# Third-block products behind X and Y, split bk transposes, filler ahead of chunk 0, modulation sums on VectorE

## The chip, the core and the metric

The kernel runs on one core of a Trainium2 chip. The metric is the device time of one execution in microseconds (us). The core has TensorE (PE, with its weight loads PEld), VectorE (DVE), ScalarE (ACT), GpSimd (POOL) and SyncE (SP, which issues the DMAs). TensorE's granted clock is shown as a share of full speed: 1.00 is 2.4 GHz, 0.50 is 1.2 GHz.

## The reference, cut to what matters

Two layers; each runs three token mixers on the same normalised input and merges them. 1024 latent and 256 context tokens, width 1024, all in float32.

```python
mod = silu(cond) @ w_mod + b_mod                       # 3072 sums for x, as many for ctx: the modulation
shift, scale, gate = split(mod, 3)
h = rms_norm(x, g) * (1 + scale) + shift               # h @ w_in gives all streams of the three mixers
# A: RWKV-7, both directions, 8 heads of 64
S_t = S_{t-1} (diag(w_t) - kk_t^T (a_t kk_t)) + v_t^T k_t ;  y_t = S_t r_t
# B: y = B * conv3(C * u)      C: differential attention, 4 heads, two softmax maps each
x = x + gate * (sum_i sigmoid(g_i) * (y_i * silu(z_i)) @ w_branch_i) @ w_out
```

## The kernel before, in words

Every large product is made of three fp32r products (high and low halves): a group of 24 products of 128x512 or 128x256 for one PSUM tile `pjt`, recorded at L158. A weight block of 256 columns arrives as two `wraw` loads, ScalarE rounds it to `whi` and VectorE subtracts to `wlo` (`split`, L111 to L113).

A layer runs in this order. `proj_stage` (L319) makes r, k, v, the decays and the q and k of attention, and ends with the conv stage (L563 to L593): four blocks `pr`, each with `u` and `cu` groups and then `gb` and `z` groups. `mod_next` (L553) is called once per token group there and works off one of 24 modulation blocks in layer 0 (8 in layer 1). One block is a 128x1024 load `wm`, eight products (L252) with `sc32` as weights that put four partial sums into four partition groups of `pjt`, a copy to `mr` on VectorE (L258), and a small product with `sel2` (L262, the fold) that adds the four, deferred behind the next group.

`rwkv_stage` (L597) is the chunked scan: 20 chunks of 64 tokens, both directions and all heads at once, on small products recorded at L148. For a chunk c:

- `prep(c, d)` (L642) makes the products `pa` of k and r with b and k, masks them to `mb` on VectorE (L656), and ScalarE copies the diagonal blocks to `dg` (L662).
- `turn_b(c)` (L664) transposes `bkT` through the PSUM tile `pt` into `bk`, four products and one ScalarE copy per direction.
- `solve(c)` (L675) inverts the unit triangular 32x32 diagonal blocks on VectorE: two transposes `dgT` and `at`, then some forty short steps on `P` and `R` (the first writes `P` at L702), and the transposes `tt` and `tn` (L720, L723).
- `corner(c)` (L729) makes the third, off-diagonal 32x32 block of the inverse: W from `mb` and `tn` on PE, a copy `ws` on ScalarE, Z from `ws` and `tt` on PE, a copy into `ti`.
- `chain(c)` (L748): X and Y products of the old state, then U from `ti` and X, then D and the second Y products, and the new state S on VectorE.

Buffers matter here. `dgT`, `R` and `tn` share one buffer (tag R); `P` and `ws` share one (tag P); W, Z and `pt` share one PSUM bank (tag pt, pool `pre`); U has a bank of its own (tag U, pool `chn`); `bk` has two buffers.

The loop (L809 to L832) interleaves the steps of chunk c with the solve of c + 1 and the preparation of c + 2. Between them `fill` (L1244) issues steps of projections that later stages need: `vd_fill`, `z_fill`, then `g_fill`, as a rule six products (a quarter of a group) per step. `PACE[l]` sets how many steps a call takes (7 in two calls, in layer 1 3 in one) and, as its third number, how many are left to attention, which spreads them over its own steps (L1256). A scheduler orders the instructions of each engine from the program, so the order below differs a little from the code. Each engine then takes its instructions in that order.

Of the kernel before, what the change touches and what calls it, by code (L numbers as in the profile page):

```python
# [23 lines left out]
FTH = 1  # L24
VDE = ((0,), ())
PJB = (0, 3)
PACE = ((7, 2, 184), (3, 1, 107))


B_LW, B_KR, B_V, B_QD, B_KD, B_VD, B_UC, B_GZ, B_ZA, B_ZC, B_G = 0, 1, 5, 7, 9, 11, 13, 17, 21, 23, 25  # L30
# [9 lines left out]
def tile_backbone(ctx: ExitStack, tc: tile.TileContext, xT_in, cond_in, w_mod, vecs, w_in, d_up, a_up,  # L40
# [88 lines left out]
    def defer(f, n=1):  # L129

        late.append([n, f])
# [108 lines left out]
        hv.append(small.tile([128, NV], F32, name=f"hv{l}"))  # L240
        ve.tensor_scalar(out=hv[l], in0=vec[l], scalar1=0.5, scalar2=None, op0=ALU.mult)

    def mod_stage(l, blocks, tags=(("wm", 1),), behind=False):
        prev = None
        for x, b in enumerate(blocks):
            ps = pj_tile()
            tag, nb = tags[x % len(tags)]
            raw = wp.tile([128, 8, 128], F32, tag=tag, name="wm", bufs=nb)
            dma.dma_start(out=raw, in_=w_mod[l, b])
            for k in range(8):  # L250
                g = k % 4
                i = te.matmul(out=ps[32 * g:32 * g + 32, 0:128], lhsT=sc32[:, k, :], rhs=raw[:, k, :],  # L252
                              start=(k < 4), stop=(k >= 4), skip_group_check=True)
            if prev is not None:
                with tc.issue_after(i.ins):
                    prev()
            mr = small.tile([128, 128], F32, tag="mr", name="mr", bufs=2)
            ve.tensor_copy(out=mr, in_=ps[:, 0:128])  # L258

            def fold(b=b, ps=ps, mr=mr):  # L260
                pm = ps[:, 128:130]
                te.matmul(out=pm, lhsT=mr, rhs=sel2, start=True, stop=True)  # L262
                m = modT[l][:, b, :]
                ve.tensor_scalar(out=m, in0=pm, scalar1=vec[l][:, V_BM + b:V_BM + b + 1], scalar2=None, op0=ALU.add)
                if 8 <= b < 16:
                    ve.tensor_scalar(out=G[l][:, b - 8, :], in0=m, scalar1=1.0,
                                     scalar2=vec[l][:, V_NG + b - 8:V_NG + b - 7], op0=ALU.add, op1=ALU.mult)
                elif b >= 16:
                    ve.tensor_scalar(out=m, in0=m, scalar1=0.5, scalar2=None, op0=ALU.mult)

            if behind:
                defer(fold)
            else:
                prev = fold
        if prev is not None:
            prev()

# [41 lines left out]
    def proj_stage(l, lowp, les, w):  # L319
# [233 lines left out]
        def mod_next():  # L553
            if mods:
                m, mb_ = mods.pop(0)
                mod_stage(m, [mb_], behind=True)

        hvl = hv[l]

# [37 lines left out]
    def rwkv_stage(l, fill):  # L597
# [63 lines left out]
                    s = slice(64 * (1 - p) + 32 * q, 64 * (1 - p) + 32 * q + 32)  # L661
                    se.copy(out=dg[s, d], in_=mb[s, d, p, :, 32 * q:32 * q + 32])  # L662

        def turn_b(c):  # L664
            if c >= 20:
                return
            bkT = bkTs.pop(c)
            bk = bks[c] = rp.tile([128, 2, 4, 128], F32, tag="bk", name="bk", bufs=2)
            for d in range(2):
                pt = pre.tile([128, 4, 128], F32, tag="pt", name="pt")  # L670
                for pr in range(4):
                    te.transpose(out=pt[:, pr, :], in_=bkT[:, 4 * d + pr, :], identity=ident)
                se.copy(out=bk[:, d], in_=pt)

        def solve(c):  # L675

# [52 lines left out]
        def corner(c):  # L729

            if c >= 20:
                return
            mb, (tt, tn) = mbs[c], tts.pop(c)
            W = pre.tile([128, 4, 128], F32, tag="pt", name="W").rearrange("p a (b i) -> p (a b) i", i=32)[:, 0:8, :]
            run_mm([(W[blk(p, 1), 4 * d + pr, :], mb[blk(p, 0), d, p, pr, 32:64], tn[blk(p, 0), 4 * d + pr, :], True, True)
                    for d, pr, p in units])
            ws = rp.tile([128, 4 * 7 * 28], F32, tag="P", name="ws", bufs=1)[:, 0:256].rearrange("p (u i) -> p u i", i=32)
            for p in range(2):
                se.copy(out=ws[blk(p, 1)], in_=W[blk(p, 1)])
            yield  # L740
            Z = pre.tile([128, 4, 128], F32, tag="pt", name="Z").rearrange("p a (b i) -> p (a b) i", i=32)[:, 0:8, :]
            run_mm([(Z[blk(p, 0), 4 * d + pr, :], ws[blk(p, 1), 4 * d + pr, :], tt[blk(p, 1), 4 * d + pr, :], True, True)
                    for d, pr, p in units])
            for p in range(2):
                se.copy(out=ti[blk(p, 0), :, 32:64], in_=Z[blk(p, 0)])
            yield

        def chain(c, S, yst):  # L748
            y, kr, mb, uv = has_y(c), krs.pop(c), mbs.pop(c), uvs[c]
            X = chn.tile([128, 2, 4, 64], F32, tag="XD", name="X")  # L750
            Y = chn.tile([128, 2, 4, 64], F32, tag="Y", name="Y") if y else None
            first = lambda d, pr: d == 0 and pr == 0
            calls = [(X[half[1 - p], d, pr, :], mb[half[p], d, p, pr, 0:64], uv[half[p], d, p, pr, :], first(d, pr), False)
                     for d, pr, p in units]
            for d, pr, p in units:
                kc, sv = kr[half[p], 4 * d + pr, :], S[half[p], d, pr, :]
                calls.append((X[half[1 - p], d, pr, :], kc[:, 0:64], sv, False, False))
                if y:

                    calls.append((Y[half[p], d, pr, :], sv, kc[:, 64:128], first(d, pr), False))  # L760
            run_mm(calls)
            x1 = rp.tile([128, 2, 4, 64], F32, tag="xs", name="xs", bufs=1)
            se.copy(out=x1, in_=X)
            yield
            U = chn.tile([128, 2, 4, 64], F32, tag="U", name="U")
            run_mm([(U[half[1 - p], d, pr, :], ti[half[1 - p], 4 * d + pr, :], x1[half[1 - p], d, pr, :], True, True)
                    for d, pr, p in units])
            for p in range(2):
                se.copy(out=uv[half[1 - p], :, p], in_=U[half[1 - p]])
            yield  # L770
            bk = bks.pop(c)
            D = chn.tile([128, 2, 4, 64], F32, tag="XD", name="D")
            calls = [(D[half[p], d, pr, :], bk[:, d, pr, half[p]], uv[:, d, p, pr, :], True, True) for d, pr, p in units]
            if y:
                calls += [(Y[half[p], d, pr, :], uv[:, d, p, pr, :], mb[:, d, p, pr, 64:128], False, True)
                          for d, pr, p in units]
            run_mm(calls)
            Sn = rp.tile([128, 2, 4, 64], F32, tag="S", name="S", bufs=2)
            ve.tensor_tensor(out=Sn, in0=D, in1=S, op=ALU.add)
            ve.tensor_tensor(out=f8(Sn), in0=f8(Sn), in1=dd_all[0][:, c, :].unsqueeze(2).to_broadcast([128, 8, 64]),  # L780
                             op=ALU.mult)
            if y:
                i = c % 2
                se.copy(out=yst[:, 0, :, 64 * i:64 * i + 64], in_=Y[:, 0])
                se.copy(out=yst[:, 1, :, 64 - 64 * i:128 - 64 * i][:, :, ::-1], in_=Y[:, 1])
                if i:
                    w = c // 2
                    for d, tb in enumerate((1024 + 128 * w if w < 2 else 128 * w - 256, 1152 - 128 * w)):
                        dma.dma_start(out=yd_dr[l][d][:, :, tb:tb + 128], in_=yst[:, d])
            uvs.pop(c)  # L790
            yield Sn
# [5 lines left out]
        load_b(1)  # L797
        load_k(1)
        load_v(0)
        for c in range(2):  # L800
            prep(c, 0)
            prep(c, 1)
            turn_b(c)
            if c == 0:
                for _ in solve(0):
                    fill()
                cor = corner(0)
                next(cor)
        load_b(2)  # L809
        for c in range(20):  # L810
            if c % 2 == 0:
                yst = rp.tile([128, 2, 4, 128], F32, tag="yst", name="yst", bufs=1)
            load_v(c + 1)
            load_k(c + 2)
            load_b(c + 3)
            steps, sol = chain(c, S, yst), solve(c + 1)
            next(steps)
            next(cor)
            next(sol, None)
            fill()  # L820
            next(steps)
            prep(c + 2, 0)
            next(sol, None)
            fill()
            S = next(steps)
            prep(c + 2, 1)
            next(sol, None)
            turn_b(c + 2)
            next(sol, None)
            fill()  # L830
            cor = corner(c + 1)
            next(cor, None)  # L832
        es.close()

    def vd_fill(l, b, sp):
# [398 lines left out]
    for l in range(NL):  # L1234
# [9 lines left out]
        def fill():  # L1244

            x, (a, b, _) = next(turns), PACE[l]
            for _ in range((x + 1) * a // b - x * a // b):
                next(both, None)
# [123 lines left out]
```

## Time and profile before

| | |
|---|---|
| median of 3 runs | 3638.03 us (3637.86 to 3639.08) |
| the profiled execution | 3636.97 us, span 3635.0 us, mean granted clock 0.986 |
| PE busy | 3486.7 us, 96% of the span |
| DVE, ACT, POOL busy | 66%, 47%, 4% |
| the rest of the span without PE | 148.3 us |

The page gives busy times of one profiled execution. Products are pipelined, so their durations overlap: what one costs is the distance from its start to the next start. A stretch is read with its busy time of each engine and its granted clock; a wait is the idle time ahead of an instruction, with what released it. The kernel is a chain of stages, so a gain counts in the stage where it falls, and only if the engine concerned is the one that sets that stage's length.

### The profile page before, as it was taken

To read this page: it belongs to the slowest core of one execution; us is meant where nothing else is said; L and a number is where in the kernel's file an instruction comes from. 1 tells how busy PE (TensorE), PEld (TensorE's weight loads), DVE (VectorE), ACT (ScalarE), POOL (GpSimd) and SP (SyncE) were. 2 spreads that over 40 slices of the span, in tenths; PEclk is the share of its full clock that TensorE was granted. 3 is DMA by queue.
4 is the path that set the end of the run, shared out by engine and by line. 5 is a ranking of instruction groups with operands and counts; after the bars stand their busy time and mean duration, and the time that the engine had idled before them with its cause. 6 is when DMAs were issued, how large, how long until landed. Compare 5 with 4: busy or idle time off the path is not lost. (4 is left out here: it accounts for less than half of the span.)

```text
span 3635.0 us, 71657 instructions
## 1 busy us (share of the span) xinstructions
PE 3486.7 (96%) x28540; PEld 2897.0 (80%) x28540; DVE 2401.8 (66%) x5166; ACT 1704.5 (47%) x3335; POOL 149.0 (4%) x418
## 2 busy tenths in 40 slices
PE   8999999989999999998999999999999999999899
PEld 5787988888888888886776777978877777888677
DVE  6736752368878587775655765733788885888572
ACT  5745221134444487765334764211444444878540
POOL 0100000000000000000000110000000000000000
PEclk8999999999999999999999999999999999999999
DMA  5546222233233323235764455231333333223473
GB/s 201 141 130 173 72 94 92 100 127 118 93 119 109 115 78 91 85 103 193 245 200 135 108 159 153 82 102 64 117 110 121 119 113 105 86 88 131 160 252 122
DMA packets 378575, 454.79 MB, mean 125 GB/s; under 512 B 119808, under 2 KB 266752, under 8 KB 378240
## 3 DMA queue, kind: packets, MB, share of 16 engines
q1 hardware_dynamic: 376320, 447.58, 38.7%
q8 instruction: 225, 3.69, 0.4%
q0 software_dynamic: 1920, 2.62, 0.4%
q14 instruction: 110, 0.90, 0.1%
HBM read 300.66 MB, written 146.80 MB: 123 GB/s over the span
## 5 line engine op out<-in xcount | busy, mean ns | idle before, releaser
L158 PE MATMUL pjt<-hT0h,whi 128*128 128x512 f32 x1488 | 556.3, 374 | 2.8 <-ACT hT0h L303 1.0
L158 PE MATMUL pjt<-hT0l,whi 128*128 128x512 f32 x1488 | 537.1, 361 | 0.9 <-DVE hT0l L304 0.7
L158 PE MATMUL pjt<-hT0h,wlo 128*128 128x512 f32 x1488 | 533.3, 359 | 0.1
L158 PE MATMUL pjt<-hT1h,whi 128*128 128x512 f32 (+1 forms) x1072 | 424.8, 396 | 5.6 <-ACT tl L338 1.6
L158 PE MATMUL pjt<-hT1l,whi 128*128 128x512 f32 (+1 forms) x1072 | 416.7, 389 | 0.3 <-issue 0.3
L158 PE MATMUL pjt<-hT1h,wlo 128*128 128x512 f32 (+1 forms) x1072 | 413.4, 386 | 1.3 <-DVE wlo L113 1.3
L112 ACT CAST whi<-wraw 128x1024 fp32r<-128x1024 f32 x208 | 218.0, 1050 | 310.9 <-PE pjt L158 282.4
L113 DVE TENSOR_TENSOR wlo<-wraw,whi 128x1024 fp32r<-128x1024 f32 x208 | 255.0, 1227 | 136.1 <-ACT whi L112 133.8
L158 PEld LDWEIGHTS pjt<-hT0h,whi 128*128 128x128 f32 x1488 | 284.2, 191 | 54.5 <-issue 10.4
L158 PEld LDWEIGHTS pjt<-hT0l,whi 128*128 128x128 f32 x1488 | 284.8, 191 | 42.4 <-issue 4.9
L158 PEld LDWEIGHTS pjt<-hT0h,wlo 128*128 128x128 f32 x1488 | 283.8, 191 | 43.2 <-issue 1.5
L954 DVE TENSOR_REDUCE mx<-s 128x1 f32<-128x512 f32 (+1 forms) x400 | 230.7, 588 | 66.0 <-PE s L952 64.6
L962 ACT ACTIVATE p<-s,mx 128x512 f32<-128x512 f32 (+1 forms) x400 | 239.1, 610 | 43.5 <-DVE mx L957 42.3
L158 PEld LDWEIGHTS pjt<-hT1h,whi 128*128 128x128 f32 x1072 | 202.2, 189 | 51.9 <-issue 7.3
L158 PEld LDWEIGHTS pjt<-hT1h,wlo 128*128 128x128 f32 x1072 | 202.3, 189 | 42.5 <-DVE wlo L113 2.5
L158 PEld LDWEIGHTS pjt<-hT1l,whi 128*128 128x128 f32 x1072 | 202.4, 189 | 41.3 <-issue 6.3
L662 ACT COPY dg<-mb 32x128 f32<-32x128 f32 x320 | 94.7, 296 | 167.0 <-DVE mb L656 161.3
L952 PE MATMUL s<-kh,qs 128*128 128x512 f32 (+1 forms) x400 | 152.0, 383 | 5.1 <-issue 3.3
L158 PE MATMUL pjt<-ya,whi 128*128 128x512 f32 (+1 forms) x448 | 136.4, 389 | 8.1 <-ACT ya L112 7.0
L712 DVE TENSOR_TENSOR P<-at,R 128x16 f32<-128x16 f32 (+6 forms) x280 | 137.6, 492 | 8.8
L714 DVE TENSOR_REDUCE R<-P 128x4 f32<-128x16 f32 (+6 forms) x280 | 136.2, 487 | 8.1
L952 PE MATMUL s<-kl,qs 128*128 128x512 f32 (+1 forms) x400 | 140.6, 354 | 0.0
(279 smaller groups left out, 7911.7 us busy)
## 6 DMA issues: line engine op xcount, KB each, us to landing
wraw<-in_w_in_dram SPq DMA_DIRECT2D x148, 512.0 KB, 4.1
kr<-kr SPq DMA_DIRECT2D x68, 512.0 KB, 3.2
wm<-in_w_mod_dram SPq DMA_DIRECT2D x48, 512.0 KB, 3.5
th<-fth SPq DMA_DIRECT2D x96, 256.0 KB, 2.0
wraw<-in_w_br_dram SPq DMA_DIRECT2D x36, 512.0 KB, 4.8
th<-th SPq DMA_DIRECT2D x64, 256.0 KB, 3.7
wraw<-in_w_out_dram SPq DMA_DIRECT2D x24, 512.0 KB, 4.2
bk<-bkt SPq DMA_DIRECT2D x80, 128.0 KB, 2.4
```

The lines of the kernel that those rows point to most:

```text
L112: se.copy(out=hi, in_=src)
L113: ve.tensor_tensor(out=lo, in0=src, in1=hi, op=ALU.subtract)
L158: i = te.matmul(out=ps, lhsT=a, rhs=b, start=(c == 0), stop=(c == n - 1))
L662: se.copy(out=dg[s, d], in_=mb[s, d, p, :, 32 * q:32 * q + 32])
L712: ve.tensor_tensor(out=pv, in0=at[:, i0:i1, i1:32].unsqueeze(2).to_broadcast([128, 4, nm, n]), in1=R[:, b + 1:8, i1:32].unsqueeze(1).to_br ...
L714: ve.tensor_reduce(out=R[:, b + 1:8, i0:i1].rearrange("p m i -> p i m"), in_=pv, axis=AX.X, op=ALU.add)
L952: te.matmul(out=s[:, :n], lhsT=qs[:, c, 128 * e:128 * e + 128], rhs=kd[c][x][:, c0:c0 + n], start=(x == 0), stop=(x == 1))
L954: ve.tensor_reduce(out=mx[:, x0:x0 + 1], in_=s[:, :n], axis=AX.X, op=ALU.max)
L962: se.activation(out=p[:, o:o + n], in_=tiles[x0][:, :n], func=AF.Exp, scale=0.125, bias=mx[:, 3:4], accum_out=sums[:, x0:x0 + 1])
```

## The change

Four things move.

1. Modulation blocks in the conv stage no longer use PE for their sums. VectorE multiplies the loaded block by `sc32`, once for each of the two conditions, and adds eight slices down to one in three halving steps; PE only adds over partitions, two products with `one32` (the new fold). The first 16 blocks, at the start of the kernel, stay as they are.
2. W and Z lie in U's bank (tag U) as one tile `WZ`. W of chunk c is issued in chunk c's own turn, behind X and Y, not at the end of the turn before; Z follows after a filler, ahead of the preparation of c + 2.
3. `turn_b` takes one direction per call: the first stands ahead of `prep(c + 2, 0)`, the second behind `prep(c + 2, 1)`.
4. One `fill` call stands ahead of chunk 0's preparation and two within it; `PACE` becomes (10, 3, 184) and (14, 5, 112).

```diff
-PACE = ((7, 2, 184), (3, 1, 107))
+PACE = ((10, 3, 184), (14, 5, 112))
...
+    def mod_behind(l, b, mp):
+
+        raw = wp.tile([128, 8, 128], F32, tag="wm", name="wm", bufs=1)
+        dma.dma_start(out=raw, in_=w_mod[l, b])
+        ma = mp.tile([128, 2, 128], F32, tag="ma", name="ma", bufs=2)
+        for ci in range(2):
+            mq = mp.tile([128, 8, 128], F32, tag="mq", name="mq", bufs=1)
+            ve.tensor_tensor(out=mq, in0=raw, in1=sc32[:, :, ci:ci + 1].to_broadcast([128, 8, 128]), op=ALU.mult)
+            ve.tensor_tensor(out=mq[:, 0:4], in0=mq[:, 0:4], in1=mq[:, 4:8], op=ALU.add)
+            ve.tensor_tensor(out=mq[:, 0:2], in0=mq[:, 0:2], in1=mq[:, 2:4], op=ALU.add)
+            ve.tensor_tensor(out=ma[:, ci], in0=mq[:, 0], in1=mq[:, 1], op=ALU.add)
+
+        def fold():
+            pm = pj_tile()[:, 0:4].rearrange("p (c e) -> p c e", e=2)
+            for ci in range(2):
+                te.matmul(out=pm[:, ci], lhsT=ma[:, ci], rhs=one32[:, 0:2], start=(ci == 0), stop=(ci == 1),
+                          skip_group_check=True)
+            mod_put(l, b, slice(0, 2), modT[l][:, b, :], pm[:, :, 0])
+
+        defer(fold)
...
-                mod_stage(m, [mb_], behind=True)
+                mod_behind(m, mb_, p1)
...
-        def turn_b(c):
+        def turn_b(c, d):
             if c >= 20:
                 return
-            bkT = bkTs.pop(c)
-            bk = bks[c] = rp.tile([128, 2, 4, 128], F32, tag="bk", name="bk", bufs=2)
-            for d in range(2):
-                pt = pre.tile([128, 4, 128], F32, tag="pt", name="pt")
-                for pr in range(4):
-                    te.transpose(out=pt[:, pr, :], in_=bkT[:, 4 * d + pr, :], identity=ident)
-                se.copy(out=bk[:, d], in_=pt)
+            if d == 0:
+                bks[c] = rp.tile([128, 2, 4, 128], F32, tag="bk", name="bk", bufs=2)
+            bkT, bk = bkTs[c], bks[c]
+            pt = pre.tile([128, 4, 128], F32, tag="pt", name="pt")
+            for pr in range(4):
+                te.transpose(out=pt[:, pr, :], in_=bkT[:, 4 * d + pr, :], identity=ident)
+            se.copy(out=bk[:, d], in_=pt)
...
-            W = pre.tile([128, 4, 128], F32, tag="pt", name="W").rearrange("p a (b i) -> p (a b) i", i=32)[:, 0:8, :]
+            WZ = chn.tile([128, 2, 8, 32], F32, tag="U", name="WZ")
+            W, Z = WZ[:, 0], WZ[:, 1]
...
-            Z = pre.tile([128, 4, 128], F32, tag="pt", name="Z").rearrange("p a (b i) -> p (a b) i", i=32)[:, 0:8, :]
...
+        fill()
         for c in range(2):
-            prep(c, 0)
-            prep(c, 1)
-            turn_b(c)
+            for d in range(2):
+                turn_b(c, d)
+                prep(c, d)
+                if c == 0:
+                    fill()
             if c == 0:
                 for _ in solve(0):
                     fill()
-                cor = corner(0)
-                next(cor)
...
-            steps, sol = chain(c, S, yst), solve(c + 1)
+            steps, sol, cor = chain(c, S, yst), solve(c + 1), corner(c)
             next(steps)
             next(cor)
             next(sol, None)
             fill()
+            next(cor)
+            turn_b(c + 2, 0)
+            prep(c + 2, 0)
             next(steps)
-            prep(c + 2, 0)
             next(sol, None)
             fill()
             S = next(steps)
             prep(c + 2, 1)
+            turn_b(c + 2, 1)
             next(sol, None)
-            turn_b(c + 2)
             next(sol, None)
             fill()
-            cor = corner(c + 1)
-            next(cor, None)
```

On PE, in the middle of layer 1's scan, the third block before: the last two rows of filler at the end of a turn, W, the X and Y products, Z, and the fillers that follow.

```order
L158 MATMUL pjt<-hT1l_21243,whi 128x512
L158 MATMUL pjt<-hT1h_21242,wlo 128x512
L148 MATMUL W<-tn,mb 32x32 x16
L148 MATMUL X<-uv,mb 64x64 x16
L148 MATMUL X<-S,kr 64x64
L148 MATMUL Y<-kr,S 64x64
...
L148 MATMUL Z<-tt,ws 32x32 x16
L158 MATMUL pjt<-hT1h_21242,whi 128x512
...
L148 MATMUL U<-xs,ti 64x64 x16
L148 MATMUL pa<-kr,bkT 128x128 x8
```

The same place after. The filler rows left out between the two WZ rows are nine more here and fifteen in most turns.

```order
L148 MATMUL X<-uv,mb 64x64 x16
...
L148 MATMUL WZ<-tn,mb 32x32 x16
L158 MATMUL pjt<-hT1h_20848,whi 128x512
L158 MATMUL pjt<-hT1l_20849,whi 128x512
L158 MATMUL pjt<-hT1h_20848,wlo 128x512
...
L148 MATMUL WZ<-tt,ws 32x32 x16
L693 MATMUL pt<-cst,bkT 128x128 x4
L148 MATMUL pa<-kr,bkT 128x128 x8
L148 MATMUL U<-xs,ti 64x64 x16
```

W moved behind X and Y, and between W and Z the fillers stand where X and Y stood; one direction's transposes and `pa` moved ahead of U.

On DVE, in the conv stage of layer 0, around the change to the next weight block (`cu` and `cv` are the conv stage's own steps, `mr` the copy for the fold, `modT` the fold's result), before:

```order
L572 TENSOR_TENSOR cu<-pjt,u 128x512
L258 COPY mr<-pjt 128x128
L582 SCALAR_TENSOR_TENSOR cv<-cu,hv_221,cv 128x512
L581 SCALAR_TENSOR_TENSOR cv<-cu,hv_221,cv 128x512
L582 SCALAR_TENSOR_TENSOR cv<-cu,hv_221,cv 128x512
L264 TENSOR_SCALAR modT_219<-pjt,vec_217 128x2
L269 TENSOR_SCALAR modT_219<-modT_219 128x2
L113 TENSOR_TENSOR wlo<-wraw,whi 128x1024
L572 TENSOR_TENSOR cu<-pjt,u 128x256
L258 COPY mr<-pjt 128x128
L113 TENSOR_TENSOR wlo<-wraw,whi 128x1024
```

and after:

```order
L602 SCALAR_TENSOR_TENSOR cv<-cu,hv_221,cv 128x512
L259 TENSOR_TENSOR mq<-wm,sc_79 128x1024
L245 TENSOR_SCALAR modT_219<-pjt,vec_217 128x2
L260 TENSOR_TENSOR mq<-mq 128x512
L250 TENSOR_SCALAR modT_219<-modT_219 128x2
L603 SCALAR_TENSOR_TENSOR cv<-cu,hv_221,cv 128x512
L261 TENSOR_TENSOR mq<-mq 128x256
L113 TENSOR_TENSOR wlo<-wraw,whi 128x1024
L593 TENSOR_TENSOR cu<-pjt,u 128x256
L262 TENSOR_TENSOR ma<-mq 128x128
L113 TENSOR_TENSOR wlo<-wraw,whi 128x1024
L259 TENSOR_TENSOR mq<-wm,sc_79 128x1024
```

Where one copy to `mr` stood, the multiply and the adds of a block stand, spread among the stage's own steps and the `wlo` steps.

## Rows read from the trace of the kernel before

**Rows 1.** The page: engines' busy time and share; PE in 40 slices, tenths.

```profile
PE 3486.7 (96%) x28540; PEld 2897.0 (80%) x28540; DVE 2401.8 (66%) x5166; ACT 1704.5 (47%) x3335; POOL 149.0 (4%) x418
PE   8999999989999999998999999999999999999899
```

**Rows 2.** Stretches: length, busy by engine, clock, DMA: conv, scan start, scans, attention.

```profile
core 0: us, PE busy (x) PEld busy (x) DVE busy (x) ACT busy (x) POOL busy (x), PEclk, DMA share, GB/s
495.00:735.00 240.00, 240.00 (x1583) 201.43 (x1583) 74.16 (x152) 37.79 (x52) 1.22 (x11) 1.00 0.28 100
735.80:764.60 28.80, 23.73 (x303) 21.84 (x301) 20.33 (x46) 8.23 (x22) 0.75 (x3) 1.00 0.40 136
764.60:1193.00 428.40, 408.51 (x6351) 350.67 (x6351) 349.81 (x849) 184.33 (x423) 36.29 (x111) 0.96 0.33 109
...
2580.80:2996.40 415.60, 392.50 (x6051) 331.32 (x6051) 349.10 (x844) 184.66 (x411) 34.82 (x109) 1.00 0.34 113
...
3094.00:3276.00 182.00, 181.86 (x1032) 151.00 (x1031) 153.07 (x374) 145.93 (x344) 0.00 (x0) 1.00 0.28 87
```

**Rows 3.** PE's waits, whole span: total us, times, longest; then one in the timeline.

```profile
PE W L148 <- DVE tn L723: 19.1, 13, 2.6
PE W L148 <- ACT bk L673: 17.1, 18, 2.1
...
764.58 1.06 PE L148 MATMUL W<-tn,mb 32*32 32x32 f32 x32 [2.58 <-DVE tn L723]
```

**Rows 4.** Timeline of DVE, layer 1's first chunk: start, length, instruction, idle before.

```profile
2581.60 0.45 DVE L681 STREAM_TRANSPOSE dgT<-dg 128x256 f32<-128x256 f32 x1 [0.87 <-PE W L148]
2582.08 1.25 DVE L685 STREAM_TRANSPOSE at<-dgT 128x1024 f32<-128x1024 f32 x1
...
2587.03 0.19 DVE L702 TENSOR_TENSOR P<-t,at 128x32 f32<-128x32 f32 x1 [3.52 <-PE Z L148]
```

**Rows 5.** Timeline of one chunk in layer 0, PE and then DVE.

```profile
862.86 0.69 PE L148 MATMUL W<-tn,mb 32*32 32x32 f32 x32 [1.21 <-ACT bk L673]
863.48 1.08 PE L148 MATMUL X<-uv,mb 64*64 64x64 f32 x29
...
865.49 0.69 PE L148 MATMUL Z<-tt,ws 32*32 32x32 f32 x32
...
866.40 0.20 DVE L702 TENSOR_TENSOR P<-t,at 128x32 f32<-128x32 f32 x1 [0.39 <-PE Z L148]
...
883.50 0.45 DVE L723 STREAM_TRANSPOSE tn<-tt 128x256 f32<-128x256 f32 x1
```

**Rows 6.** Timeline of PE: 18 fillers ahead of D, and the next W.

```profile
871.35 0.50 PE L158 MATMUL pjt<-hT0h,whi 128*128 128x512 f32 x1
...
875.68 1.15 PE L148 MATMUL D<-uv,bk 128*64 128x64 f32 x32
...
885.32 0.69 PE L148 MATMUL W<-tn,mb 32*32 32x32 f32 x32
```

**Rows 7.** Two stretches at half clock, layers 0 and 1 (columns as rows 2).

```profile
764.50:771.30 6.80, 6.72 (x59) 6.44 (x60) 1.80 (x4) 4.23 (x10) 1.25 (x4) 0.50 0.00 0
...
2669.10:2672.50 3.40, 3.40 (x38) 2.73 (x38) 2.56 (x9) 1.39 (x3) 0.00 (x0) 0.50 0.00 0
```

**Rows 8.** Timeline of PE in the conv stage: a modulation block and a fold.

```profile
504.62 0.39 PE L158 MATMUL pjt<-hT0h,wlo 128*128 128x512 f32 x1
504.93 0.64 PE L252 MATMUL pjt<-wm,sc 128*32 128x128 f32 x16
505.51 0.39 PE L158 MATMUL pjt<-hT0h,whi 128*128 128x256 f32 x1
...
508.49 0.28 PE L262 MATMUL pjt<-cst,mr 128*128 128x2 f32 x2
508.63 0.36 PE L158 MATMUL pjt<-hT0h,whi 128*128 128x256 f32 x1
```

**Rows 9.** Groups by line and shape: busy us, mean ns | idle before, releaser.

```profile
L656 DVE TENSOR_TENSOR mb<-pa,cst 128x1024 f32<-128x1024 f32 x72 | 87.2, 1211 | 9.3 <-PE pa L148 9.3
L779 DVE TENSOR_TENSOR S<-D,S 128x512 f32<-128x512 f32 x40 | 27.3, 683 | 9.4 <-PE D L148 9.4
L258 DVE COPY mr<-pjt 128x128 f32<-128x128 f32 x48 | 13.7, 285 | 62.2 <-PE pjt L252 62.2
L113 DVE TENSOR_TENSOR wlo<-wraw,whi 128x1024 fp32r<-128x1024 f32 x208 | 255.0, 1227 | 136.1 <-ACT whi L112 133.8 <-DMA v<-kk 1.3
```

More of the change, by code (lines that the diff above doesn't have):

```diff
@@ L241, in tile_backbone, with mod_put, mod_stage @@
         ve.tensor_scalar(out=hv[l], in0=vec[l], scalar1=0.5, scalar2=None, op0=ALU.mult)
-    def mod_stage(l, blocks, tags=(("wm", 1),), behind=False):
+    def mod_put(l, b, ci, m, pm):
+        ve.tensor_scalar(out=m, in0=pm, scalar1=vec[l][:, V_BM + b:V_BM + b + 1], scalar2=None, op0=ALU.add)
+        if 8 <= b < 16:
+            ve.tensor_scalar(out=G[l][:, b - 8, ci], in0=m, scalar1=1.0,
+                             scalar2=vec[l][:, V_NG + b - 8:V_NG + b - 7], op0=ALU.add, op1=ALU.mult)
+        elif b >= 16:
+            ve.tensor_scalar(out=m, in0=m, scalar1=0.5, scalar2=None, op0=ALU.mult)
+    def mod_behind(l, b, mp):
[15 more added lines that the diff above has]
+        defer(fold)
+    def mod_stage(l, blocks, tags=(("wm", 1),)):
         prev = None
@@ L262, in fold @@
                 te.matmul(out=pm, lhsT=mr, rhs=sel2, start=True, stop=True)
[L263 to L274, printed above, removed]
+                mod_put(l, b, slice(0, 2), modT[l][:, b, :], pm)
+            prev = fold
         if prev is not None:
@@ L748, in chain @@
         def chain(c, S, yst):
-            y, kr, mb, uv = has_y(c), krs.pop(c), mbs.pop(c), uvs[c]
+            y, kr, mb, uv = has_y(c), krs.pop(c), mbs[c], uvs[c]
             X = chn.tile([128, 2, 4, 64], F32, tag="XD", name="X")
```

## The prediction

> **What bounds the kernel now.** The profiled execution took 3636.97 us (span 3635.0), 1.1 us under the median of 3638.03; I sum against it. First the page: PE is busy 96% of the span, at 9 tenths in nearly every slice [rows 1]. A change therefore pays where it removes PE work, or PE idle time that nothing refills. Then the stretches [rows 2]: the conv stage of layer 0 keeps PE busy 240.0 of 240.0 us, with VectorE (DVE) at 74.2; attention is equally full (181.9 of 182). The two scan loops (18 chunk periods each, from the first W to the 19th) are not: 408.5 of 428.4 us in layer 0, at a granted clock of 0.96, and 392.5 of 415.6 in layer 1. Then the waits of PE: W waits for tn (19.1 us) and for the copies of pt to bk (17.1) [rows 3].
>
> Last the timeline of a chunk, because DVE runs a closed circle there. Its rows: dgT starts once W is done (R holds tn until then), at follows, and the first P waits until Z is done, since ws lies in P's buffer [rows 4]. In the second layer's first chunk Z came late and P sat idle 3.52 us for it [rows 4]. From the first P to the end of tn a chunk took 17.55 us (866.40 to 883.95) [rows 5], with one 256-wide fth (0.33 net) in it: 17.2. Over the chunks I find 17.1 where other work stands in it, 16.4 where none does. So, start of W to start of next W:
> DVE path = W 0.62 + what stands between W and Z + Z 0.62 + 0.21 lag + 17.1 (16.4) + fth and wlo placed after P + 0.15.
> Before, X and Y stand between W and Z: 2.0 us (863.48 to 865.49 [rows 5]). With 1.3 us of fth and wlo per chunk the path is 21.9. PE's own path is 22.5 with 66 filler products and no wait (W at 862.86, next at 885.32 [rows 5, 6]), some 21 to 22 with 60 or 54. The two paths meet at W each chunk; they are near equal, and neither alone is the bound. Longer of both, chunk by chunk: 403 and 401 us. The excess (25 and 15) is the bk waits, small lags (about 0.3 a chunk where DVE is longer), and in layer 0 the clock: granted half (0.50) right after W waited 2.58 us [rows 3, 7], and in five more stretches, 34 us in all, so up to 17 us lost.
>
> **Modulation sums.** Removed: per block 8 products (16 matrix instructions), 32 blocks (24 + 8). One stands between products started at 504.62 and 505.51: 0.89 less the 0.23 of a normal step is 0.66 us [rows 8]. The fold was 0.14 (508.49 to 508.63); now it is two such, so 0.14 is given back. Net 0.52, or 0.58 with the slower restart of the next product: 32 x 0.55 = 17.6 us, all of it on PE's path since PE has no idle time there.
> Added on DVE: per block two chains of 1024, 512, 256 and 128 elements. Rows: 1211 and 683 ns for 1024 and 512, 285 for a 128-wide copy [rows 9]; 256 lies between these, and I take 0.41. With 0.04 between chained steps (dgT to at [rows 4]) that is 5.5 us a block, 132 in layer 0, less 7 for the copies to mr: 74 + 125 = 199 us of DVE in a stage that would last 228. The cover holds at 87%, but thinly: wlo (1227 ns [rows 9]) of the next weight block now queues behind a multiply, with eight block changes in layer 0 and as many in layer 1 (lighter there). I charge 2.5 us; bounds 0 (no stall seen before) and 12 (a whole multiply at ten changes). The next block's weight load waits on SP until DVE's second multiply and the later wraw loads stand behind it; with four PSUM buffers in that stage and a block period of 9.5 us against 5.5 I charge nothing.
> A page of the Trainium skill speaks against this part: "VectorE: DVE Perf Modes", section The DRAIN you can't avoid, says that after each operation a flush of about its duration less 266 ns passes before the next starts, so that one should have few operations. By it (an estimate with the durations above) a block costs 8.2 us and the stage would be DVE's, 264 us. The rows do not bear it out: at starts 0.03 us after dgT ends [rows 4]. I keep it as a rival.
>
> **W behind X and Y.** Gone: every wait of W for bk (17.1 us), as WZ shares no bank with pt, and W's waits for tn shrink by X's 2.0 us where PE was early. New: what stands between W and Z. The order shows 18 (sometimes 12) filler products there in place of X and Y. Eighteen at 512 columns take 4.33 us (871.35 to 875.68 [rows 6]); with the 256-wide groups of layer 0 the mean is 3.3, in layer 1 3.4. P waits for Z, hence the DVE path grows by 1.3 to 1.4 us a chunk, minus what of wlo and fth the scheduler puts ahead of P (0.5 a chunk, mean). Counting the extras that the order leaves behind P (1.1 and 1.3): 0.62 + 3.3 + 0.62 + 0.21 + 16.9 + 1.1 + 0.15 = 22.9, and 23.2 in layer 1. PE's path falls to 21.1 and 20.8 (60 and 50 fillers in place of 63 and 53). So DVE becomes the longer in 33 of 36 chunks, and PE stands at W for tn instead of bk. Longer of both, summed: 416 and 417 us. Lag of 0.3 a chunk: 5 each. Clock: 8 chunks per layer leave PE a gap of 2 us or more at W; such gaps were followed by half clock most times (layer 1 had one such stretch [rows 7], after a wait of 2.4). I take 8 in 10, and 1.3 us each, since W and the fillers ahead of Z then run slow, and those are on DVE's path: 8 us a layer; bounds 0 and 14.
> Layer 0: 416 + 5 + 8 = 429 against 428.4: +1. Layer 1: 417 + 5 + 8 = 430 against 415.6: +14.5.
>
> **Split bk transposes.** The same eight products and two copies; only the place moves. bk has two buffers, and the copy of the first half waits for D, on ScalarE behind both uv copies, so pt stays full until then. Nothing but the second half waits for it. The copies of dg now stand between the two uv copies; D can start some 6 us after Z, against 2.6 plus the second 18 fillers (2.2 to 4.3): up to 1.3 us of PE idle in a few chunks, inside DVE's longer path. Charged nothing; 5 us if the DVE path should not bind.
>
> **Filler ahead of chunk 0 and PACE.** From the end of the conv products to the first W took 28.8 us in layer 0, 23.7 busy [rows 2]. After: 16 steps of 12 products at 0.126 (24.2) plus 8.0 of small products = 32.2 us; the solve's own chain allows 31.4. So +3.4, with six steps more done. The steps in all stay 220 in layer 0. Tail and attention: about 0 net. In layer 1 the start does not change; 184 steps instead of 189 are done in the scan, and five move to attention, which is full [rows 2]: 5 x 6 x 0.23 = +6.8, less 0.8 in the tail: +6. What they leave in the scan is worth nothing, since DVE is the longer there.
>
> **Sum.** Conv -17.6 + 2.5 = -15; layer 0 +1 + 3.4 = +4.5; layer 1 +14.5 + 6 = +20.5. Together +10: 3637 + 10 = 3647, and 3648 beside the median.
>
> **Rivals.**
> 1. Faster: the same circle, without its by-costs. If DVE's fillers fit into the wait ahead of P (it offers 1.2 to 2.3 us) and the clock holds, the lags and dips go (-13 per layer) and extras shrink: 3648 - 26 = 3622. For: layer 1's scan ran nearly all of its time at full clock [rows 2] although W waited there often. Against: the waits at W become longer, not shorter. It decides where PE's waits at W stay under about 2 us.
> 2. The conv stage turns to VectorE: by the page's flush 264 us instead of 229, or because DVE falls behind the weight blocks: 3648 + 35 = 3683. For: 87% is little room. Against: chained steps follow within 0.04 us.
> 3. It does not do what I say: P is not held by Z, so PE's path binds, 380 and 375 plus 0.35 a chunk: the scans lose 42 and 34 us, 3560. Against: the 3.52 us wait [rows 4], and the order keeps Z behind the fillers.
>
> **How the numbers follow.** A measurement of this kernel tells 0.2% (7.3 us) from no change. Forecast 0.54: 3648, own range 3638 to 3664; a quarter of it falls within 0.2%. Rival 1 0.31: 3622, range 3612 to 3640, a third of it within 0.2%. Rival 2 0.11, rival 3 0.04. Slower: 0.41 + 0.11 = 0.52. Same: 0.13 + 0.10 = 0.23. Faster: 0.21 + 0.04 = 0.25. The range from 3617 to 3670 leaves out rival 3, most of rival 2 and the low end of rival 1.
>
> **What would show it.** Right: the wait of W for bk gone and for tn grown to 40 us or more; P idle before its first step for Z, 1 to 3 us a chunk; scan loops at 429 and 430; conv of layer 0 near 229 with DVE at 195 to 200; half-clock stretches in both scans. Wrong: a loop under 405 us (DVE is not the circle), a conv stage at 240 or more (stalls took the products' room), or W without waits.

## The result, and the profile after

The changed kernel takes 3660.80 us (median of 4 runs, 3655.88 to 3667.78) against 3638.56 before: a ratio of 1.0063, 95% interval 1.0045 to 1.0081, slower and clear of noise. The profiled execution took 3655.88 us, 18.9 more than that of before (3636.97). A second set of runs gave 3664.47 against 3640.76 (experiment 1). Two executions far out of line, one of the kernel before (6741.83 us) and one of experiment 8 (11953.58), are left out of all ratios.

The page, engines' busy time and PE in 40 slices, beside [rows 1]: PE's work fell by 8.8 us, DVE's grew by 147.8.

```profile
PE 3477.9 (95%) x28092; PEld 2902.1 (79%) x28092; DVE 2549.6 (70%) x5390; ACT 1705.7 (47%) x3335; POOL 153.8 (4%) x418
PE   8999999998999999998999999999998999999899
```

The stretches beside [rows 2] (conv stage of layer 0, its end to the first W, the loops of 18 chunks of layers 0 and 1, and all of layer 1 behind the scan); columns as there:

```profile
495.00:725.00 230.00, 229.05 (x1275) 200.13 (x1273) 185.04 (x321) 38.24 (x53) 1.59 (x19) 1.00 0.33 107
726.10:757.70 31.60, 29.95 (x336) 28.19 (x336) 21.53 (x47) 10.82 (x23) 3.74 (x6) 0.95 0.41 137
757.70:1190.80 433.10, 400.67 (x6416) 341.66 (x6410) 348.59 (x849) 182.86 (x424) 34.47 (x105) 0.98 0.33 106
2579.80:3016.70 436.90, 401.33 (x6154) 337.72 (x6154) 350.93 (x846) 184.84 (x411) 36.45 (x109) 0.97 0.33 107
3051.70:3650.00 598.30, 580.80 (x2878) 467.53 (x2876) 416.35 (x861) 350.36 (x718) 0.00 (x0) 0.99 0.44 141
```

The conv stage got shorter as meant, with DVE now busy in 200 of its 230 us. Both loops got longer although they hold fewer fillers (the projection products that `fill` issues; 1080 and 1047 recorded in the loops of the two layers, 1125 and 1063 before): in layer 1 PE idles 35.6 us of 436.9, where it idled 23.1 of 415.6. Cut at the first `pt` product of each scan, the first W, the 19th W, the last Y and the end of PE's last product, the whole difference is:

| stretch | before | after | difference | predicted |
|---|---|---|---|---|
| start to first `pt` (with conv of layer 0) | 736.9 | 726.1 | -10.8 | -15 with the conv of layer 1 |
| first `pt` to first W | 27.7 | 31.6 | +3.9 | +3.4 |
| loop, layer 0 | 428.4 | 433.1 | +4.7 | +1 |
| rest of that scan | 36.6 | 37.0 | +0.4 | 0 |
| on to layer 1's first `pt` (with its conv) | 1325.9 | 1327.4 | +1.5 | see the first row |
| `pt` to first W, layer 1 | 25.3 | 24.7 | -0.6 | 0 |
| loop, layer 1 | 415.6 | 436.8 | +21.3 | +14.5 |
| rest of that scan, and on to PE's last product | 634.9 | 633.4 | -1.5 | +6 |
| sum | | | +18.9 | +10 |

PE's waits, whole span (engine, line, what released it: total us, times, longest), beside [rows 3]:

```profile
PE WZ L148 <- DVE tn L744: 67.4, 35, 3.6
...
PE tr L556 <- DVE ro L549: 4.4, 4, 3.1
```

and the wait of DVE's first P, same columns, before and after:

```profile
DVE P L702 <- PE Z L148: 32.3, 27, 4.9
```

```profile
DVE P L723 <- PE WZ L148: 69.6, 26, 5.0
```

The waits of W for bk are gone (17.1 before). In their place W waits for tn in 35 of 40 chunks, and the waits of P for Z have more than doubled. The 18th chunk of layer 0 shows the circle. First DVE, then PE, in the timeline (start, length, instruction, idle before):

```profile
1164.82 0.45 DVE L744 STREAM_TRANSPOSE tn<-tt 128x256 f32<-128x256 f32 x1
1166.43 0.45 DVE L702 STREAM_TRANSPOSE dgT<-dg 128x256 f32<-128x256 f32 x1 [1.17 <-PE WZ L148]
1166.91 1.25 DVE L706 STREAM_TRANSPOSE at<-dgT 128x1024 f32<-128x1024 f32 x1
...
1173.39 0.20 DVE L723 TENSOR_TENSOR P<-t,at 128x32 f32<-128x32 f32 x1 [5.05 <-PE WZ L148]
...
1190.29 0.45 DVE L744 STREAM_TRANSPOSE tn<-tt 128x256 f32<-128x256 f32 x1
```

```profile
1165.32 1.07 PE L148 MATMUL WZ<-tn,mb 32*32 32x32 f32 x32 [3.51 <-DVE tn L744]
...
1167.33 0.63 PE L158 MATMUL pjt<-hT0l,whi 128*128 128x512 f32 x1
...
1172.16 0.39 PE L158 MATMUL pjt<-hT0h,wlo 128*128 128x512 f32 x1
1172.48 0.69 PE L148 MATMUL WZ<-tt,ws 32*32 32x32 f32 x32
```

PE stood 3.51 us for tn. W then ran at half clock (1.07 us against 0.69), and so did the first fillers behind it (0.63 us each against 0.39). `at` was done at 1168.16, but P started at 1173.39, after 5.05 us of waiting for Z, since Z stood behind 16 fillers. The clock in that stretch (columns as above, the clock is the third number from the end):

```profile
1164.50:1171.30 6.80, 5.99 (x44) 4.86 (x45) 2.50 (x5) 1.66 (x4) 1.57 (x4) 0.50 0.02 8
```

From the start of W to the start of Z it took 7.16 us with these 16, and 4.93 in the chunks with 18 of the same width at full clock. In 34 of the 38 solves that run beside a Z, P starts 0.10 to 0.22 us after Z's end; in some of them a `wlo` or `fth` step ahead of P had filled part or all of the time until then.

### The profile page after: what moved, and what is told of

It is laid out like the page before. It is cut to its first block, busy times and chain, and to the rows that moved or that the text cites. A ratio compares the mean times of both kernels' runs of the same rounds, so it can differ in the third digit from the quotient of the medians.

```text
span 3654.1 us, 70943 instructions
## 1 busy us (share of the span) xinstructions
PE 3477.9 (95%) x28092; PEld 2902.1 (79%) x28092; DVE 2549.6 (70%) x5390; ACT 1705.7 (47%) x3335; POOL 153.8 (4%) x418
## 3 DMA queue, kind: packets, MB, share of 16 engines
q0 software_dynamic: 1920, 2.62, 0.4%
## 4 chain that ended last, share of the span: by engine, by line
PE 64%; DVE 23%; ACT 5%; issue 4%; DMA 3%; SPq 0%; DVEq 0%; ACTq 0%
PE pjt L158 47%; PE s L974 4%; PE o L158 3%; DVE P L733 3%; DVE R L735 3%; PE at L1007 2%; DVE mb L677 2%; DVE wlo L113 2%; DVE P L737 2%; DVE R L739 2%; PE WZ L148 1%; DVE P L723 1%; DVE t L725 1%; DMA ra<-o 1%; ACT whi L112 1%
```

## The experiments

The theory: the scan is longer because P, which shares its buffer with `ws`, waits for Z, and Z now stands behind fillers. Its rivals: the clock alone, PE's own path, or the bank. All times are device times beside the kernel before on the same chip; a loop is 18 chunks, from the first W to the 19th.

**1. The changed kernel once more** (no edit).

> The changed kernel itself, once more, for a second trace and more times. Theory A (VectorE's circle through Z sets every chunk, and half-clock stretches come on top): loops of 18 chunks less their clock loss (length times one less the granted clock) at 423 in both layers as in the first trace (433.1 less 10.2, 436.8 less 13.7), the loss itself anywhere from 7 to 20 us a layer; 3655 to 3668 us. Rival B (the loops' length is an accident of one execution): 423 missed by more than 4 us in a layer.

3664.47 us, ratio 1.0068 (1.0047 to 1.0089). The two loops:

```profile
756.70:1193.10 436.40, 403.89 (x6413) 343.52 (x6410) 348.50 (x849) 182.94 (x424) 34.63 (x105) 0.97 0.33 105
2585.40:3022.30 436.90, 401.12 (x6154) 337.57 (x6153) 351.04 (x846) 184.94 (x411) 36.56 (x109) 0.97 0.34 107
```

Length times (1 - clock), with the clock unrounded, is taken here as what the clock cost. It is 13.7 us in each, so 422.7 and 423.2 remain, where the first trace left 422.8 and 423.2. Theory A: the length at full clock repeats to 0.1 us, and what varies is the clock. By the same measure the loops of the kernel before are 413.1 and 413.9. So at full clock the change made both loops 9.7 and 9.3 us longer; the rest of the +4.7 and +21.3 in the table is the clock (5.1 us less lost in layer 0, 12.0 more in layer 1).

**2. `ws` in a buffer of its own**, in the changed kernel.

```diff
-            ws = rp.tile([128, 4 * 7 * 28], F32, tag="P", name="ws", bufs=1)[:, 0:256].rearrange(...)
+            ws = rp.tile([128, 256], F32, tag="ws", name="ws", bufs=1).rearrange(...)
```

> The changed kernel with ws in a buffer of its own, so that P no longer waits for Z. Theory A (the circle of VectorE is longer by the wait of P for Z, which stands behind 12 to 18 fillers): P starts 1.8 us after W ends instead of 4.9 on the mean, VectorE's path falls from about 24 to 21 us a chunk, PE's own path of 21 to 22 binds, loops of 18 chunks at 390 to 396 in both layers, waits of W for tn under 25 us, 3570 to 3585 us. Rival B (the scan is longer because the granted clock falls after waits, or because PE's own path grew): loops stay within 10 us of 433 and 437, 3640 or more.

3583.42 us, ratio 0.9850 (0.9836 to 0.9864): one buffer turns the change from 0.6% slower into 1.5% faster. A chunk on DVE, then on PE:

```profile
915.22 0.44 DVE L702 STREAM_TRANSPOSE dgT<-dg 128x256 f32<-128x256 f32 x1
915.69 1.25 DVE L706 STREAM_TRANSPOSE at<-dgT 128x1024 f32<-128x1024 f32 x1
917.03 0.09 DVE L707 MEMSET at<- 128x32 f32 x1
917.22 0.19 DVE L723 TENSOR_TENSOR P<-t,at 128x32 f32<-128x32 f32 x1
...
935.98 0.45 DVE L744 STREAM_TRANSPOSE tn<-tt 128x256 f32<-128x256 f32 x1
```

```profile
914.25 0.69 PE L148 MATMUL WZ<-tn,mb 32*32 32x32 f32 x32
...
917.89 0.69 PE L148 MATMUL WZ<-tt,ws 32*32 32x32 f32 x32
...
936.75 0.69 PE L148 MATMUL WZ<-tn,mb 32*32 32x32 f32 x32
```

P starts 2.0 us after dgT and before Z; tn is done 0.3 us before W starts. W's waits for tn fall from 67.4 us to 15.7. The circle is the cause: theory A, and its time. Its loops were missed, though: 406.1 and 404.6 instead of 390 to 396 (columns as above).

```profile
754.40:1160.40 406.00, 394.42 (x6411) 338.19 (x6408) 348.46 (x849) 182.28 (x423) 34.86 (x108) 0.99 0.35 112
2543.40:2948.00 404.60, 394.04 (x6152) 334.09 (x6151) 348.74 (x845) 183.73 (x409) 37.74 (x111) 0.98 0.36 114
```

PE's own period, in chunks of layer 0 without idle time, is mostly 21.2 or 22.5 us with 60 fillers; I had taken 21.1 and 20.8.

**3. The filler behind Z**, `ws` and P still in one buffer.

```diff
-            fill()
             next(cor)
+            fill()
             turn_b(c + 2, 0)
```

> The changed kernel with the first filler call of a turn behind Z instead of between W and Z; ws and P still share a buffer. Theory A (it is the filler between W and Z that costs): Z starts 0.85 us after W ends (two ws copies of 0.74 in all), P is ready some 1.8 us after W, PE idles 0.85 us a chunk ahead of Z, loops 395 to 408, 3585 to 3605 us. Rival B (VectorE's path is not set by Z): loops unchanged within 10 us and PE's new idle on top, 3660 or more.

3592.72 us, ratio 0.9870 (0.9853 to 0.9887), loops 409.0 and 404.6: theory A, with layer 0's loop 1 us over its range.

```profile
893.23 0.69 PE L148 MATMUL WZ<-tn,mb 32*32 32x32 f32 x32
893.85 0.50 PE L158 MATMUL pjt<-hT0h,whi 128*128 128x512 f32 x1
...
894.97 0.69 PE L148 MATMUL WZ<-tt,ws 32*32 32x32 f32 x32
```

The scheduler left a few fillers there while `ws` was copied, so PE hardly idled (2.8 us of waits of Z for `ws` in all). The wait of P for Z, 69.6 us in all, is 2.1 here. Two unlike edits, one of the buffer and one of the order, give the same loops to 3 us.

**4. `ws` in a buffer of its own in the kernel before** (the edit of experiment 2).

> The kernel before with ws in a buffer of its own. Theory A (in the kernel before the two paths are near equal, VectorE's held by Z behind X and Y): VectorE's path falls by about 1 us a chunk, the waits of W for tn (19.1 us) nearly go, those for the bk copy (17.1) stay or grow, loops 400 to 410 in layer 0 and 392 to 402 in layer 1, 3590 to 3615 us. Rival B (PE's own path with the bk waits is the bound there): loops within 5 us of 428 and 416, 3632 to 3640.

3636.62 us, ratio 0.9990 (0.9978 to 1.0001), loops 420.5 and 420.7. PE's waits:

```profile
PE W L148 <- ACT bk L673: 26.4, 21, 2.8
PE W L148 <- DVE tn L723: 13.0, 7, 2.9
```

Rival B by the time, though the loops moved by -8 and +5. The waits for tn fell from 19.1 to 13.0 us, and those for bk took the room (17.1 to 26.4): together 36.2 before, 39.4 here. Less clock loss the loops are 413.7 and 413.9 (before 413.1 and 413.9): what moved them was the clock, and the buffer alone moves neither by more than 0.6 us.

**5. W and Z in U's bank, in the old order**: only the tile `WZ` of the diff.

> The kernel before with W and Z in U's bank at their old places, ws and P still in one buffer. Theory A (the circle through Z binds as soon as the bk waits go): waits for bk gone, waits for tn up to 25 to 40 us, loops within 8 us of 428 and 416, 3628 to 3642 us. Rival B (the bank alone was the obstacle): loops under 412 and 405, 3615 or less.

3625.76 us, ratio 0.9961 (0.9949 to 0.9974). The bk waits are gone:

```profile
PE WZ L148 <- DVE tn L723: 24.5, 20, 2.9
```

Loops 419.4 and 411.6. W's waits for tn grew to 24.5 us, just under theory A's 25 to 40, and the time is 2 us under its range and far above rival B's: the bank frees more than the circle takes back. That P's wait for Z is short in the old order (22.8 us, longest 1.7, with X and Y between W and Z) fits this, but no run separates it. This part of the change, by itself, is worth 0.4%.

**6. Both, in the old order**: U's bank and `ws` in its own buffer.

> The kernel before with two edits: W and Z in U's bank at their old places in the order, and ws in a buffer of its own. Theory A (two obstacles stand at W, the pt bank and the circle through Z; each alone leaves the other as the bound): the 26 us of waits of W for bk are gone, waits for tn at 10 to 25 us, loops at 403 to 412 in layer 0 and 398 to 408 in layer 1, 3600 to 3615 us. Rival B (the new order of the change, not the bank, removes the wait, and U's bank brings a wait of its own: W has to wait for the uv copies of U): W's waits stay at 30 us or more, 3625 to 3640.

3623.60 us, ratio 0.9955 (0.9938 to 0.9973), no different from experiment 5; loops 416.6 and 412.3, both theories missed. Z now waits for ScalarE:

```profile
PE WZ L148 <- DVE tn L723: 16.0, 11, 2.9
...
PE WZ L148 <- ACT ws L740: 9.9, 9, 2.3
```

The loops stay 10.5 and 7.7 us above those of experiment 2, but hold more filler: 1142 and 1076 recorded products against 1080 and 1047. At 0.23 us from start to start for 512 columns and 0.12 for 256, the 62 of layer 0 (all of 256) are 7.4 us and the 29 of layer 1 (18 of 512) 5.5. So most of that difference is work that was moved, and the new order, with its `PACE`, gains outside the loops as well (from the 19th W to the last Y 31.5 and 32.6 us, against 36.3 and 35.1). How much of that is the order and how much `PACE` was not separated.

**7. `tn` in its own buffer, `ws` in that of `dg`**, in the changed kernel, dgT ahead of W.

```diff
-            tn = rp.tile([128, 8, 32], F32, tag="R", name="tn", bufs=1)
+            tn = rp.tile([128, 8, 32], F32, tag="tn", name="tn", bufs=1)
...
-            ws = rp.tile([128, 4 * 7 * 28], F32, tag="P", name="ws", bufs=1)[:, 0:256].rearrange(...)
+            ws = rp.tile([128, 2, 4, 32], F32, tag="dg", name="ws", bufs=1).rearrange(...)
...
-            next(cor)
             next(sol, None)
+            next(cor)
```

> The changed kernel with tn in a buffer of its own and ws in that of dg, whose blocks dgT has read by then; dgT stands ahead of W. VectorE's solve then needs nothing of PE but the masks. Theory A (with ws free PE's own path binds, VectorE still holds W in a few chunks): waits of W for tn under 12 us, loops 396 to 404, 3565 to 3580 us. Rival B (PE's path is all that is left): within 4 us of the version with ws alone set free, 3579 to 3588. Rival C (dg taken later holds the preparation of c + 2 up): 3590 or more.

3619.56 us, ratio 0.9945 (0.9928 to 0.9962), loops 427.1 and 416.0: rival C by the time, though not by its way. W has next to no wait for tn left (0.2 us), and D waits in its place:

```profile
PE D L148 <- ACT uv L790: 41.6, 21, 4.9
```

The timeline of ScalarE names it:

```profile
1022.99 0.58 ACT L790 COPY uv<-U 64x512 f32<-64x512 f32 x1 [2.02 <-PE U L148]
1026.38 1.22 ACT L683 COPY dg<-mb 32x128 f32<-32x128 f32 x4 [2.81 <-DVE mb L677]
1027.61 0.58 ACT L790 COPY uv<-U 64x512 f32<-64x512 f32 x1
```

The four dg copies stand between the two uv copies. They wait 2.81 us for the masks `mb` from DVE, which runs steps of the solve until 1025.08, and the second uv copy, whose U products ended at 1022.95, waits behind them. So in this chunk it is the masks that are late, not the buffer of dg. "TensorE: Matmul & The Clock Gate" of the Trainium skill says, in the table at its head, that ScalarE takes its queue strictly in order; this trace agrees (1027.61, right behind the copy that ended at 1027.60).

**8. The modulation sums alone**, in the kernel before (the diff's `mod_behind`, nothing else).

> The kernel before with the modulation sums of layer 0's and layer 1's conv stages on VectorE, nothing else changed. Theory A (the removed products are worth 0.55 us a block on PE's path and VectorE's cover holds): conv of layer 0 shorter by 11 to 15 us, conv of layer 1 by 3 to 5, scans unchanged, so 3620 to 3626 us. Rival B (layer 1 gives nothing, as the changed kernel's stages seem to say: its conv 179.0 against 180.1): 3626 to 3630. Rival C (VectorE holds the conv stage up): 3635 or more.

3631.78 us, ratio 0.9970 (0.9958 to 0.9983), 9 us under before by the medians. Against the kernel before that is rival B's gain (8 to 13 us; theory A had 12 to 19). By the stages layer 0 gave what A says (first `cu` to first `pt` 242.4 to 229.9), and layer 1 less than its 3 to 5 (180.1 to 177.8, and 178.9 in the changed kernel). DVE's groups in the changed kernel (busy us, mean ns | idle before, releaser):

```profile
L259 DVE TENSOR_TENSOR mq<-wm,sc 128x1024 f32<-128x1024 f32 x64 | 78.3, 1223 | 37.4 <-DMA wm<-in_w_mod_dram 27.2 <-DMA k<-qt 8.9
L260 DVE TENSOR_TENSOR mq<-mq 128x512 f32<-128x512 f32 x64 | 44.0, 688 | 1.1
L261 DVE TENSOR_TENSOR mq<-mq 128x256 f32<-128x256 f32 x64 | 27.0, 421 | 1.2
L262 DVE TENSOR_TENSOR ma<-mq 128x128 f32<-128x128 f32 x64 | 18.5, 289 | 1.4
```

These are 2.62 us a chain and 5.2 a block; I had 5.5. In layer 1 the last `tr` product (a transpose for attention, ahead of the conv stage) waits for DVE, in all traces with the sums on DVE:

```profile
2366.40 0.87 PE L556 MATMUL tr<-cst,ro 128*128 128x128 f32 x3 [3.06 <-DVE ro L549]
```

```profile
2366.00:2372.80 6.80, 5.68 (x15) 4.34 (x16) 2.42 (x4) 1.17 (x2) 0.36 (x8) 0.50 0.12 40
```

Before, nine more products stood ahead of that `tr` on PE and its waits for `ro` were 0.5 us at the longest. The scheduler, given other instructions, put those nine behind it: 3.06 us of wait, and half clock after it. What this costs in all was not measured by itself.

**9. All but the sums**: the changed kernel with the modulation back on TensorE.

> The changed kernel with the modulation sums of the conv stages back on TensorE: the scan edits and PACE alone. Theory A (the parts add, and vector sums are worth 8 to 15 us): conv of layer 0 at 242 to 243 us, scans at 422 to 424 less clock loss as with the whole change, 3669 to 3679 us, 0.8% to 1.1% above the kernel before. In layer 1 the wait of the last tr product for ro (3.06 us, with the clock at half behind it) goes back to under 1 us. Rival B (the vector sums cost elsewhere what they save in the conv stage): 3655 to 3667.

3672.28 us, ratio 1.0083 (1.0058 to 1.0109): theory A. The parts add: -0.30% (experiment 8) and +0.83% make +0.53%, beside 0.63% and 0.68% for the whole. The wait of `tr` is back to what it was:

```profile
PE tr L535 <- DVE ro L528: 1.3, 3, 0.5
```

Its loops less clock loss are 422.5 and 424.2, those of the whole change.

**10. The bk transposes together again**, on the version of experiment 2: both `turn_b` calls ahead of the turn's last solve step.

```diff
-            turn_b(c + 2, 0)
             prep(c + 2, 0)
...
             prep(c + 2, 1)
-            turn_b(c + 2, 1)
             next(sol, None)
+            turn_b(c + 2, 0)
+            turn_b(c + 2, 1)
             next(sol, None)
```

> The version with ws in its own buffer, and both directions' bk transposes together again at their old place, ahead of the turn's last solve step. Theory A (the split is worth nothing, since nothing but the second half waits for the first copy): within 5 us of 3583. Rival B (the split saves what PE waits for the copy between the two halves, some 0.5 us a chunk in 36 chunks): 3595 or more.

3587.33 us, ratio 0.9851 (0.9824 to 0.9877), loops 404.5 and 403.3: theory A by the median. The split is worth nothing that these runs can tell; their interval leaves room for some 10 us either way.

**11. U ahead of the preparation of c + 2**, on the version of experiment 2.

```diff
-            prep(c + 2, 0)
             next(steps)
+            prep(c + 2, 0)
```

> The version with ws in its own buffer, and the preparation of c + 2, first direction, behind U as in the kernel before. Theory A (the dg copies then stand behind both uv copies on ScalarE, so D no longer waits for uv, 7.5 us in that version): 3573 to 3582. Rival B (U right behind Z waits for the two ti copies, 0.74 us plus lags in 36 chunks, which pa had covered): 3588 to 3610.

3590.68 us, ratio 0.9855 (0.9828 to 0.9881), loops 404.6 and 404.0. The wait of D for uv (7.5 us) left the list of PE's waits, as A says, but the loops gained 1.5 and 0.6 us only, and less clock loss nothing (401.6 and 398.9, in experiment 2 401.5 and 397.8). The median lies in rival B's range, but its interval overlaps that of experiment 2 and the loops show none of B's cost, so neither theory's size is right. No version is told to be faster than that of experiment 2, 1.5% under the kernel before.

## Why the prediction was right, and where its terms were off

- **The circle of DVE: right, in mechanism and size.** At full clock I had 421 (416 and 5) and 422 (417 and 5) us for the loops; the traces leave 423 in each, twice. The signs came: W waits 67.4 us for tn (I said 40 or more), P waits 69.6 us in all, 1.7 a chunk on the mean of 40 (1 to 3), half clock in both scans; with the clock the loops are 4 and 7 us over the 429 and 430 I gave. Experiments 2 and 3 show the cause from two sides. Rival 1, that the circle would shed its by-costs, is out: the loops grew by 9 to 10 us at full clock and lost more to the clock than I charged.
- **The clock term was mis-sized.** I took 8 dips of 1.3 us, at 8 in 10, for 8 us a layer. There were 5 stretches in layer 0 and 6 in layer 1, fewer than that, but they lost 10.2 and 13.7 us, 2.0 to 2.3 each, since some last 6.8 us. That is 7.9 us more than I charged; my sum was 9 short of the profiled execution, and the other errors nearly cancel. That they do is luck: the terms of layer 1's blocks and of its attention, below, were off by +5.9 and -7.5 us (measured less forecast). The clock is also why layer 1 lost so much more than layer 0: before, the loop of layer 0 had lost 15.3 us by the same measure, that of layer 1 only 1.7.
- **The conv stage of layer 0: right, its size in part by chance.** -10.8 where 24 of 32 blocks made -13.2, with 2.5 of stalls -10.7; DVE at 200 us, as forecast. From its first `cu` the stage itself got 12.6 us shorter (242.4 to 229.8), so, if the blocks were worth their 13.2, the stalls were under 1 us and not 2.5; the first `cu` came 1.8 us later (496.3 for 494.5), which makes the -10.8. The rival that DVE sets this stage is out. So is, for these steps, the flush that the prediction took from "VectorE: DVE Perf Modes", section The DRAIN you can't avoid, of the Trainium skill: by my estimate from it the stage would be 264 us, and it took 230. The section itself adds that a next operation which is not held starts earlier; here `at` started 0.03 us after dgT ended (1166.91 after 1166.88).
- **Layer 1's blocks (-4.4) were costed at their place alone.** The stage itself got 1.2 us shorter (180.1 to 178.9), and ahead of it the order moved nine products at the last `tr`, 3.06 us of wait and half clock after it. The whole stretch from the last Y to layer 1's first `pt` got 1.5 us longer; less clock loss it is the same (1317.4 and 1317.2). The step that failed is "removed, so saved": I did not look at where the scheduler put the neighbours. Why the stage itself gave so little stays open.
- **Layer 1's attention (+6) was wrong.** I read it as full off one stretch of 182 us [rows 2]. Over all that follows the scan PE idled 22.5 of 599.0 us before, in this row (columns as above), and 17.5 of 598.3 after; the five extra steps went into that at no cost.

```profile
3032.00:3631.00 599.00, 576.48 (x2854) 460.54 (x2852) 412.96 (x858) 348.35 (x716) 0.00 (x0) 0.99 0.43 139
```

  In the traces with 112 steps left to attention that stretch is 596.7 to 601.8 us long, in those with 107 598.5 to 604.8.
- **Split transposes and the start: right** (0, within what experiment 10 can tell, and +3.9 for +3.4; 1.7 us of the 3.9 is clock loss, which I had not charged there).
- **What I left out of the sum is the largest number here.** I costed fillers between W and Z at 1.3 us a chunk against the old order and stopped there. With P free of Z (experiment 2) the loops took 406.1 and 404.6 us instead of 433.1 and 436.8: 59 us of the two loops stood behind one shared buffer, some 47 of it at full clock and 12 in clock loss. My third rival (P not held) had its place, but with PE's path too short: 3560 where experiment 2 gave 3583.

The median lies 22 us above before, the profiled execution 19: it was the fastest of the four, at a mean clock of 0.983, the others at 0.980 and 0.981.

## What to carry to other kernels

Before moving work between two steps of one engine, look for who else waits for the second of them through a shared buffer: here twelve or eighteen fillers, in most chunks, were put ahead of Z, and a solve on another engine stood behind Z only because a scratch tile had the same tag. When one wait is removed, find the next one on the same instruction first; the bank alone was worth 0.4%, the buffer alone nothing that can be told, the new order (and its `PACE`) with the bank a loss of 0.8%, and all three with the sums 1.5%. A removed instruction saves its time only if the order around it stays: compare the order at the neighbouring waits too.

## What the runs showed of the hardware

- The run-to-run spread of this kernel goes with its clock. Over the runs of the kernel before that the ratios use, the time went from 3629.91 us at a mean granted clock of 0.988 to 3652.13 at 0.981; the lost 0.007 of 3640 us is 25 us, and they differ by 22. The changed kernel's eight runs, at 0.983 to 0.980, lie between 3655.88 and 3671.10.
- A wait does not cost its length alone. With the wait of 3.51 us shown above, which ended at 1165.32, the granted clock stood at half from 1164.50 to 1171.30, and since W and the fillers ahead of Z ran in that stretch, the circle of DVE got at least 2.2 us longer (from W to Z 7.16 with 16 fillers, for 4.93 with 18 at full clock; W itself 1.07 for 0.69). So a circle that makes PE wait slows itself down: clock losses of the loops were 10.2 to 13.7 us with the circle, 4.6 and 6.8 in experiment 2. The kernel before shows that other waits do the same: 15.3 us in layer 0, after a first wait of 2.58 us at W, and 1.7 in layer 1.
- Chained DVE steps of one block (multiply and three adds) ran at 200 us of busy time in 230 with next to no hold on PE: its idle time in that window was 0.95 us.
